# Layer 1's FFN tail: Silu and the activations' high parts written to PSUM, and the second half's norm moved into the FFN tiles

## The chip, the core and the metric

The kernel runs on one core of a Trainium2 chip. Its engines are PE (TensorE, the matmuls; PEld is its weight loading), DVE (VectorE), ACT (ScalarE), POOL (GpSimd) and SP (SyncE, which here only issues transfers). They run side by side and wait for one another through semaphores; each executes its own instructions in the order written. SBUF is the large on-chip memory, PSUM the small one into which PE accumulates; DVE and ACT read and write both. The metric is the time of one execution on the device in microseconds (us), the median over several runs.

## The reference

Two layers of a hybrid attention block over 1024 tokens of width 1024. What matters here is the end of layer 1: the residual after attention's output projection, an RMS norm with gain and shift, and a SwiGLU FFN with inner width 2816 (22 blocks of 128).

```python
def _swiglu(h, wg, wu, wd):
    return (jax.nn.silu(h @ wg) * (h @ wu)) @ wd
...
        x = x + g1 * o
        h = _rms(x, norm2_g[i]) * (1.0 + sc2) + sh2
        x = x + g2 * _swiglu(h, ffn_w_gate[i], ffn_w_up[i], ffn_w_down[i])
```

All of it is float32, and the kernel keeps that precision with split operands.

## The kernel before

**Split matmuls.** Every operand is split into a high part (a cast to a shorter format) and a low part (the source minus the high part). `mm3` multiplies high x high (L74), low x high (L75) and high x low (L76) into one PSUM tile. So each operand costs a cast on ACT, a subtraction and three matmuls for each product. In the rows w_hi, w_lo are a weight's parts, c_hi, c_lo the normed input's, act_hi, act_lo the activations', and h_hi, h_lo (in the program h1_hi, h1_lo, whose room is used again) hold parts of the down weights.

**Layer 1's tail.** The tokens are worked on in two halves (`ci`) of 512. `out_proj1(0)` and `out_proj1(1)` compute the output projection and the residual x, eight output blocks each. `norm1s` is a generator that computes one half's norm in small steps, which other code advances: squares on ACT, their sum (L1285), the reciprocal root (`norm_rstd`), then for each of eight blocks nrm_t (L1293) and nrm_h (L1295). own0 is the first half's, own1 the second's. own0's results go through `combine`, which makes the inputs of a Strassen-like scheme: seven products in place of eight. own1's results are kept in a DRAM tile h_d (L1401) and are read and combined when the second half begins.

**One FFN tile** (`gate_up1`) makes 128 inner columns for 512 tokens. Four weight pieces b11, b12, b21, b22 of gate and up are loaded; POOL makes the sums t1, t2 (L1328, L1329), t3 (L1343) and t4 (L1347). Seven products (`product7`) run in this order, with weights b11, t2, t3, t1, t4, b21, b22. Each is 12 matmuls of 256 columns into a p_ps buffer, of which there are three. For six of the weights `parts_of` casts w_hi on ACT (L1240), copies it to a PSUM tile pmisc on ACT (L1244) and subtracts on DVE (w_lo, L1245), so that DVE reads one operand from SBUF and one from PSUM. b22's w_lo is POOL's. pmisc has two buffers in all. DVE adds the products up into u2, u3, sg and av; ACT applies Silu in place to u3 (L1357) and sg (L1362); DVE multiplies (L1360, L1366); then act_hi is cast on ACT (L1368) and act_lo subtracted on DVE (L1369).

**The down projection.** `down_weights1(f)` loads two pieces on POOL's queue (L1383), casts on ACT (L1384) and subtracts on POOL (L1385). After each even tile from f = 2 to 18, `down1` takes the tiles f - 2 and f - 1: eight output blocks, each six matmuls of 512 columns into a d_ps buffer (three buffers), and DVE adds the result to x (L1394). The last two pairs of a half come after its loop.

**What sets the order.** In this part no order is written by hand: the framework's scheduler takes the program as written and decides each engine's order and the use of the pools' buffers. A tile of a pool can be written when the readers of the tile before it in that buffer are done. The pools here: raw weights 8, w_hi and w_lo 6 each, t 4 (shared with the norm's squares and products), raw down weights 4, act_hi and act_lo 4 each.

Of the kernel before, what the change touches and what calls it, by code (L numbers as in the profile page):

```python
# [9 lines left out]
F32 = mybir.dt.float32  # L10
F32R = mybir.dt.float32r
AF = mybir.ActivationFunctionType
ALU = mybir.AluOpType
# [3 lines left out]
P = 128  # L17
# [46 lines left out]
def build(tc, io):  # L64
    nc = tc.nc
# [3 lines left out]
    def fl(ap):  # L69
        return ap.bitcast(F32)  # L70
# [41 lines left out]
    def vec(l, which):  # L112
        return mod[l][:, which * KT:(which + 1) * KT, :]
# [1110 lines left out]
    wk, wk_cm = pools.open("wk1")  # L1224
# [27 lines left out]
    def out_proj1(ci, ready, own, side=iter(()), then=lambda: None):  # L1252

        h_hi, h_lo = h_out[ci]
        for dt in reversed(range(KT)):
            ws, old = ready
            ready = out_weights(dt - 1) if dt else then()
            ps = pd.tile([P, 512], F32, name="d_ps")
            for k in range(KT):
                hi, lo = ws[k // 4]  # L1260
                mm3(ps, hi[:, k % 4], lo[:, k % 4], h_hi[:, k], h_lo[:, k], k == 0, k == KT - 1)
            cols = slice(ci * 32, ci * 32 + 32)
            for i in range(2):
                rows = slice(8 * i, 8 * i + 8)
                V.scalar_tensor_tensor(
                    x[:, dt, ci * 512:ci * 512 + 512].rearrange("p (c r) -> p c r", r=GH)[:, :, rows],
                    ps.rearrange("p (c r) -> p c r", r=GH)[:, :, rows], vec(1, 2)[:, dt, 0:1],
                    old[i].rearrange("p (r c) -> p r c", c=GW)[:, :, cols].rearrange("p r c -> p c r"),
                    ALU.mult, ALU.add)
            advance(own, 1)  # L1270
            advance(side, 3)
        return ready

    def norm1s(ci, adder, done):


        ts = slice(ci * 512, ci * 512 + 512)
        ss = wk.tile([P, 512], F32, name="nrm_ss")
        for i, k in enumerate(reversed(range(KT))):
            if i == 0:  # L1280
                S.activation(ss, x[:, k, ts], AF.Square)
            else:
                sq = wk.tile([P, 512], F32, name="nrm_sq", tag="t", bufs=4)
                S.activation(sq, x[:, k, ts], AF.Square)
                adder.tensor_tensor(ss, ss, sq, ALU.add)  # L1285
            yield
        for r in norm_rstd(ss, 512, wk, ph):
            yield
        for i in range(4):
            both = []  # L1290
            for k in (i, i + 4):
                t = wk.tile([P, 512], F32, name="nrm_t", tag="t", bufs=4)
                V.scalar_tensor_tensor(t, x[:, k, ts], nA[3][:, k, 0:1], r, ALU.mult, ALU.mult)  # L1293
                h = wk.tile([P, 512], F32, name="nrm_h", tag="wd", bufs=4)
                S.activation(h, t, AF.Identity, bias=vec(1, 3)[:, k, 0:1], scale=1.0)  # L1295
                both.append(h)
                yield
            done(i, *both)
            yield
# [32 lines left out]
    def gate_up1(f, side=iter(()), raws=None):  # L1332
        b11, b12, b22, b21 = raws[:4] if raws else load_gate_up(f)
        t1, t2 = raws[4:] if raws else first_sums(b11, b12, b22)
        t3, t4 = (wk.tile([P, 4, P], F32, name=n, tag="t", bufs=4) for n in ("t3", "t4"))
        p1, u2, u3, sg = (wk.tile([P, HT], F32, name=n) for n in ("p1", "u2", "u3", "sg"))
        av = wk.tile([P, 2, HT], F32, name="av", bufs=2)
        hi, lo = (wk.tile([P, 512], F32R, name=n, bufs=4) for n in ("act_hi", "act_lo"))
        w = parts_of(b11)
        ps = product7(w, 0)  # L1340
        S.copy(p1, ps)
        w = parts_of(t2)
        G.tensor_tensor(t3, b22, b12, ALU.subtract)  # L1343
        ps = product7(w, 4)
        V.tensor_tensor(u2, ps, p1, ALU.add)
        w = parts_of(t3)
        G.tensor_tensor(t4, t2, b21, ALU.subtract)  # L1347
        ps = product7(w, 5)
        V.tensor_tensor(u3, ps, u2, ALU.add)
        w = parts_of(t1)  # L1350
        ps = product7(w, 3)
        V.tensor_tensor(av[:, 1], ps, u3, ALU.add)
        V.tensor_tensor(u2, ps, u2, ALU.add)
        w = parts_of(t4)
        ps = product7(w, 2)
        V.tensor_tensor(u3, u3, ps, ALU.subtract)
        S.activation(u3, u3, AF.Silu)  # L1357
        w = parts_of(b21)
        ps = product7(w, 1)
        V.tensor_tensor(av[:, 1], av[:, 1], u3, ALU.mult)  # L1360
        V.tensor_tensor(sg, ps, p1, ALU.add)
        S.activation(sg, sg, AF.Silu)  # L1362
        w = parts_of(b22, G)
        ps = product7(w, 6)
        V.tensor_tensor(u2, ps, u2, ALU.add)
        V.tensor_tensor(av[:, 0], u2, sg, ALU.mult)  # L1366
        avf = av.rearrange("p a n -> p (a n)")
        S.copy(hi, avf)  # L1368
        V.tensor_tensor(lo, avf, fl(hi), ALU.subtract)  # L1369
        advance(side, 2)  # L1370
        return hi, lo

# [23 lines left out]
                nc.scalar.dma_start(io["out"][:, dt, ts], x[:, dt, ts])  # L1396
            amid(dt)

    def keep(i, h0, h4):
        for k, h in ((i, h0), (i + 4, h4)):  # L1400
            nc.scalar.dma_start(h_d[:, k], h)  # L1401

    own0 = norm1s(0, G, combine)
    ready = out_proj1(0, out_weights(KT - 1), own0, then=lambda: out_weights(KT - 1))
    pools.close(bg_cms[0])
    cc, cc_cm = pools.open("comb", side="right")
    c_hi = cc.tile([P, 7, 4, HT], F32R, name="c_hi")
    c_lo = cc.tile([P, 7, 4, HT], F32R, name="c_lo")
    own1 = norm1s(1, V, keep)
    def first_tile():  # L1410
        raws = load_gate_up(0)
        return *raws, *first_sums(*raws[:3])

    ready = out_proj1(1, ready, own1, own0, then=first_tile)
    advance(own0, 99)
    for ci in range(2):
        acts = {}
        for f in range(NF):
            acts[f] = gate_up1(f, own1 if f else iter(()), ready if f + ci == 0 else None)
            down_weights1(f)  # L1420
            if f % 2 == 0 and 2 <= f < NF - 2:
                down1(ci, (f - 2, f - 1), [acts.pop(f - 2), acts.pop(f - 1)], False)

        h_in = []
        for i in range(4 if ci == 0 else 0):
            if i:
                h_in.append([raw_half(h_d[:, k]) for k in (i, i + 4)])
            else:
                h_in.append([wk.tile([P, 512], F32, name="h_in", tag=t) for t in ("nrm_ss", "nrm_r")])
                for h, k in zip(h_in[0], (0, 4)):  # L1430
                    nc.sync.dma_start(h, h_d[:, k])

        def amid(i):
            if h_in and i in (3, 7, 9, 12):
                combine(4 - len(h_in), *h_in.pop(0), tags=("t", "t"))

        for f in (NF - 4, NF - 2):
            down1(ci, (f, f + 1), [acts.pop(f), acts.pop(f + 1)], f == NF - 2,
                  lambda dt, f=f: amid(dt + (KT if f == NF - 2 else 0)))
# [113 lines left out]
```

## Time and profile before

| | |
|---|---|
| median of 3 runs | 2943.0 us (2942.56 to 2944.94) |
| profiled execution | 2949.19 us, span 2947.4 us |
| mean granted TensorE clock | 0.986 |
| busy over the span | PE 95%, DVE 54%, ACT 41%, POOL 27% |
| layer 1's tail | 2101 to 2947 us |

The profile is of one execution. Rows of groups give a source line, engine, operation, output and inputs with shapes and the count; then busy time and the mean length of one in ns; then the engine's idle time just before these instructions and what ended most of it. Rows of the timeline give the start and length of one instruction, and in brackets the idle time before it. Two successive matmuls overlap, so PE's rate is read from their starts. Two tiles and one down projection (a pair, or unit) repeat through the tail.

### The profile page before, as it was taken

What the parts mean: (1) busy time and instruction counts of PE and PEld (TensorE: products, weight loads), DVE (VectorE), ACT (ScalarE), POOL (GpSimd) and SP (SyncE); (2) the same over time, 40 slices, a digit from 0 to 9 for tenths busy, and PEclk for the clock granted to TensorE, in tenths of its full rate; (3) what the DMA queues carried; (4) which work ended last, traced back from release to release, by engine and by line L of the source; (5) the groups of instructions that cost most, each with busy time, mean ns of one, the idle gap of its engine ahead of it and who ended that gap; (6) DMA issues with size and microseconds to landing.
All of it is one profiled execution on the core that took longest, in us unless ns stands there. A gap on an engine that the chain in (4) does not pass through costs nothing. (4 is left out here: it accounts for less than half of the span.)

```text
span 2947.4 us, 44547 instructions
## 1 busy us (share of the span) xinstructions
PE 2812.9 (95%) x16874; PEld 2350.1 (80%) x16874; DVE 1592.2 (54%) x3144; ACT 1219.9 (41%) x2402; POOL 799.0 (27%) x870
## 2 busy tenths in 40 slices
PE   7989999999999999999989999999989899989999
PEld 5876768888888888888857778777768788888898
DVE  5775553633323333333575252566566777877776
ACT  4345552421111111111253231566447666666664
POOL 1122332000000000000130001455246666676662
PEclk9989999999999999999989999999999999999999
DMA  7236564211011110110124335876343322233231
GB/s 277 85 118 231 213 210 148 65 43 36 29 50 36 36 43 29 43 43 29 54 79 142 108 105 153 186 182 145 117 150 118 128 98 100 99 136 100 97 104 47
DMA packets 149349, 310.59 MB, mean 105 GB/s; under 512 B 13424, under 2 KB 71280, under 8 KB 142096
## 3 DMA queue, kind: packets, MB, share of 16 engines
q1 hardware_dynamic: 133664, 265.73, 28.9%
q0 software_dynamic: 8992, 31.40, 3.3%
q10 hardware_dynamic: 6480, 10.63, 1.0%
q8 instruction: 133, 2.18, 0.3%
q14 instruction: 80, 0.66, 0.1%
HBM read 264.58 MB, written 43.12 MB: 104 GB/s over the span
## 5 line engine op out<-in xcount | busy, mean ns | idle before, releaser
L74 PE MATMUL p_ps<-c_hi,w_hi 128*128 128x256 f32 x1232 | 344.6, 280 | 13.6 <-ACT w_hi L1240 4.6
L76 PE MATMUL p_ps<-c_hi,w_lo 128*128 128x256 f32 x1232 | 343.0, 279 | 4.5 <-DVE w_lo L1245 3.5
L75 PE MATMUL p_ps<-c_lo,w_hi 128*128 128x256 f32 x1232 | 342.7, 278 | 0.0
L810 POOL TENSOR_TENSOR nrm_ss<-nrm_ss,nrm_sq 128x512 f32<-128x512 f32 (+1 forms) x31 | 39.4, 1271 | 1012.9 <-PE d_ps L76 935.4
L775 ACT CAST w_hi<-w_raw 128x1024 fp32r<-128x1024 f32 x106 | 110.5, 1051 | 485.1 <-PE d_ps L75 270.4
L74 PEld LDWEIGHTS p_ps<-c_hi,w_hi 128*128 128x128 f32 x1232 | 233.7, 190 | 17.5 <-ACT w_hi L1240 6.6
L76 PEld LDWEIGHTS p_ps<-c_hi,w_lo 128*128 128x128 f32 x1232 | 233.5, 190 | 5.8 <-DVE w_lo L1245 4.5
L75 PEld LDWEIGHTS p_ps<-c_lo,w_hi 128*128 128x128 f32 x1232 | 233.6, 190 | 0.9
L580 POOL TENSOR_SCALAR pr<-pr,st 128x640 f32<-128x640 f32 (+2 forms) x208 | 156.9, 755 | 266.7 <-DVE st L579 176.8
L878 DVE SCALAR_TENSOR_TENSOR x<-d_ps,mod,x 128x512 f32<-128x512 f32 (+1 forms) x240 | 157.6, 661 | 125.2 <-PE d_ps L76 125.2
L776 DVE TENSOR_TENSOR w_lo<-w_raw,w_hi 128x1024 fp32r<-128x1024 f32 x102 | 124.1, 1224 | 184.0 <-ACT w_hi L775 181.6
L862 DVE TENSOR_TENSOR sg<-sg,u_ps 128x512 f32<-128x512 f32 (+1 forms) x66 | 39.6, 599 | 322.4 <-PE u_ps L76 322.4
L74 PE MATMUL d_ps<-act_hi,w_hi 128*128 128x512 f32 (+1 forms) x528 | 188.8, 358 | 3.5 <-DVE x L878 3.4
L75 PE MATMUL d_ps<-act_lo,w_hi 128*128 128x512 f32 (+1 forms) x528 | 188.7, 357 | 1.3 <-DVE act_lo L864 1.3
L75 PE MATMUL u_ps<-o_lo,w_hi 128*128 128x512 f32 (+1 forms) x528 | 189.3, 358 | 0.0
L76 PE MATMUL u_ps<-o_hi,w_lo 128*128 128x512 f32 (+1 forms) x528 | 189.1, 358 | 0.0
L74 PE MATMUL u_ps<-o_hi,w_hi 128*128 128x512 f32 (+1 forms) x528 | 189.0, 358 | 0.0
L76 PE MATMUL d_ps<-act_hi,w_lo 128*128 128x512 f32 (+1 forms) x528 | 188.9, 358 | 0.0
L74 PE MATMUL g_ps<-o_hi,w_hi 128*128 128x512 f32 (+1 forms) x528 | 188.2, 357 | 0.0
L75 PE MATMUL g_ps<-o_lo,w_hi 128*128 128x512 f32 (+1 forms) x528 | 188.2, 356 | 0.0
L76 PE MATMUL g_ps<-o_hi,w_lo 128*128 128x512 f32 (+1 forms) x528 | 188.2, 356 | 0.0
L574 ACT ACTIVATE pr<-sm,st 128x640 f32<-128x640 f32 (+4 forms) x208 | 162.9, 783 | 31.1 <-POOL sm L563 22.3
(329 smaller groups left out, 7494.6 us busy)
## 6 DMA issues: line engine op xcount, KB each, us to landing
ada_w<-ada_w SPq DMA_DIRECT2D x48, 1024.0 KB, 4.9
wd_raw<-w_down POOLq DMA_DIRECT2D x88, 256.0 KB, 2.9
w_raw<-w_gate SPq DMA_DIRECT2D x88, 256.0 KB, 2.6
w_raw<-w_up SPq DMA_DIRECT2D x88, 256.0 KB, 2.7
k<-k_d SPq DMA_DIRECT2D x28, 640.0 KB, 10.5
w_raw<-w_in SPq DMA_DIRECT2D x24, 512.0 KB, 4.0
w_raw<-w_gate SPq DMA_DIRECT2D x22, 512.0 KB, 3.5
w_raw<-w_up SPq DMA_DIRECT2D x22, 512.0 KB, 3.5
```

The costliest lines, as they stand in the source:

```text
L74: TE.matmul(out, lh, rh, start=first, stop=False)
L75: TE.matmul(out, lh, rl, start=False, stop=False)
L76: TE.matmul(out, ll, rh, start=False, stop=last)
L574: S.activation(self.pr[:, :n], self.sm[:, :n], AF.Exp, bias=st[:, 0:1], scale=-1.0, accum_out=st[:, 1:2])
L580: G.tensor_scalar(self.pr[:, :n], self.pr[:, :n], st[:, 3:4], 0.0, ALU.mult, ALU.add)
L775: S.copy(hi, raw)
L776: eng.tensor_tensor(lo, raw, fl(hi), ALU.subtract)
L810: adder(i).tensor_tensor(ss, ss, sq, ALU.add)
L862: V.tensor_tensor(sg[:, :n], sg[:, :n], u_ps[:, :n], ALU.mult)
L878: V.scalar_tensor_tensor(xs, self.shaped(ps[:, :n]), vec(l, 5)[:, dt, v:v + 1], xs, ALU.mult, ALU.add)
```

## The change

Three things are edited.

First, in `gate_up1` both Silus write to pmisc tiles in PSUM, and the two products that make av read them from there. act_hi is copied to a further pmisc tile by ACT (`first`), and act_lo is computed from the copy. So a tile asks for nine pmisc tiles, where it asked for six; the two buffers remain.

Second, own1 is not advanced in `out_proj1(1)` any more, only in the FFN tiles from f = 1 on, two steps a tile. Its sums and its products are POOL's (they were DVE's), the gain is applied as the scale of ACT's nrm_h, nrm_h gets one buffer of its own, and each result is written to h_d at once.

Third, the down weights of f = 0 are fetched and split together with those of f = 1.

```diff
@@ -1271,7 +1271,7 @@
             advance(side, 3)
         return ready
 
-    def norm1s(ci, adder, done):
+    def norm1s(ci, tag, bufs, each, done):
 
 
         ts = slice(ci * 512, ci * 512 + 512)
@@ -1282,7 +1282,7 @@
             else:
                 sq = wk.tile([P, 512], F32, name="nrm_sq", tag="t", bufs=4)
                 S.activation(sq, x[:, k, ts], AF.Square)
-                adder.tensor_tensor(ss, ss, sq, ALU.add)
+                G.tensor_tensor(ss, ss, sq, ALU.add)
             yield
         for r in norm_rstd(ss, 512, wk, ph):
             yield
@@ -1290,9 +1290,13 @@
             both = []
             for k in (i, i + 4):
                 t = wk.tile([P, 512], F32, name="nrm_t", tag="t", bufs=4)
-                V.scalar_tensor_tensor(t, x[:, k, ts], nA[3][:, k, 0:1], r, ALU.mult, ALU.mult)
-                h = wk.tile([P, 512], F32, name="nrm_h", tag="wd", bufs=4)
-                S.activation(h, t, AF.Identity, bias=vec(1, 3)[:, k, 0:1], scale=1.0)
+                h = wk.tile([P, 512], F32, name="nrm_h", tag=tag, bufs=bufs)
+                if ci:
+                    G.tensor_tensor(t, x[:, k, ts], r, ALU.mult)
+                else:
+                    V.scalar_tensor_tensor(t, x[:, k, ts], nA[3][:, k, 0:1], r, ALU.mult, ALU.mult)
+                S.activation(h, t, AF.Identity, bias=vec(1, 3)[:, k, 0:1], scale=nA[3][:, k, 0:1] if ci else 1.0)
+                each(k, h)
                 both.append(h)
                 yield
             done(i, *both)
@@ -1354,19 +1358,23 @@
         w = parts_of(t4)
         ps = product7(w, 2)
         V.tensor_tensor(u3, u3, ps, ALU.subtract)
-        S.activation(u3, u3, AF.Silu)
+        s2 = ph.tile([P, 512], F32, name="pmisc")[:, 0:HT]
+        S.activation(s2, u3, AF.Silu)
         w = parts_of(b21)
         ps = product7(w, 1)
-        V.tensor_tensor(av[:, 1], av[:, 1], u3, ALU.mult)
+        V.tensor_tensor(av[:, 1], av[:, 1], s2, ALU.mult)
         V.tensor_tensor(sg, ps, p1, ALU.add)
-        S.activation(sg, sg, AF.Silu)
+        s1 = ph.tile([P, 512], F32, name="pmisc")[:, 0:HT]
+        S.activation(s1, sg, AF.Silu)
         w = parts_of(b22, G)
         ps = product7(w, 6)
         V.tensor_tensor(u2, ps, u2, ALU.add)
-        V.tensor_tensor(av[:, 0], u2, sg, ALU.mult)
+        V.tensor_tensor(av[:, 0], u2, s1, ALU.mult)
         avf = av.rearrange("p a n -> p (a n)")
         S.copy(hi, avf)
-        V.tensor_tensor(lo, avf, fl(hi), ALU.subtract)
+        first = ph.tile([P, 512], F32, name="pmisc")
+        S.copy(first, fl(hi))
+        V.tensor_tensor(lo, avf, first, ALU.subtract)
         advance(side, 2)
         return hi, lo
 
@@ -1396,28 +1404,29 @@
                 nc.scalar.dma_start(io["out"][:, dt, ts], x[:, dt, ts])
             amid(dt)
 
-    def keep(i, h0, h4):
-        for k, h in ((i, h0), (i + 4, h4)):
-            nc.scalar.dma_start(h_d[:, k], h)
-
-    own0 = norm1s(0, G, combine)
+    def nothing(*a):
+        pass
+
+    own0 = norm1s(0, "wd", 4, nothing, combine)
     ready = out_proj1(0, out_weights(KT - 1), own0, then=lambda: out_weights(KT - 1))
     pools.close(bg_cms[0])
     cc, cc_cm = pools.open("comb", side="right")
     c_hi = cc.tile([P, 7, 4, HT], F32R, name="c_hi")
     c_lo = cc.tile([P, 7, 4, HT], F32R, name="c_lo")
-    own1 = norm1s(1, V, keep)
+    own1 = norm1s(1, "nrm_ss", 1, lambda k, h: nc.scalar.dma_start(h_d[:, k], h), nothing)
     def first_tile():
         raws = load_gate_up(0)
         return *raws, *first_sums(*raws[:3])
 
-    ready = out_proj1(1, ready, own1, own0, then=first_tile)
+    ready = out_proj1(1, ready, iter(()), own0, then=first_tile)
     advance(own0, 99)
     for ci in range(2):
         acts = {}
         for f in range(NF):
             acts[f] = gate_up1(f, own1 if f else iter(()), ready if f + ci == 0 else None)
-            down_weights1(f)
+            if f:
+                for i in range(0 if f == 1 else f, f + 1):
+                    down_weights1(i)
             if f % 2 == 0 and 2 <= f < NF - 2:
                 down1(ci, (f - 2, f - 1), [acts.pop(f - 2), acts.pop(f - 1)], False)
 
```

The scheduler moves far more than the edits. Three places show it, all in the first half's tiles. Numbers behind names tell tiles of one name apart.

The first is POOL, from the end of a down block in the repeating units. Before, with the current tile's pieces w_raw_21186 to 21192 (b22 is 21190), the next tile's 21362 to 21368 and the one after that 21602 to 21608:

```order
L1385 TENSOR_TENSOR h1_hi_14611<-wd_raw_21774,h1_hi_14611 128x512
L1383 DMA wd_raw_22190<-w_down 128x512
L1245 TENSOR_TENSOR w_lo_21334<-w_raw_21190,w_hi_21333 128x512
L1328 TENSOR_TENSOR t1_21610<-w_raw_21604,w_raw_21602 128x512
L1329 TENSOR_TENSOR t2_21611<-w_raw_21606,t1_21610 128x512
L1343 TENSOR_TENSOR t3_21614<-w_raw_21606,w_raw_21604 128x512
L1347 TENSOR_TENSOR t4_21615<-t2_21611,w_raw_21608 128x512
```

After, with the current tile's pieces 22078 to 22084 (b22 is 22082) and the next tile's 22258 to 22264:

```order
L1393 TENSOR_TENSOR h1_hi_14611<-wd_raw_22678,h1_hi_14611 128x512
L1391 DMA wd_raw_23098<-w_down 128x512
L1332 TENSOR_TENSOR t1_22266<-w_raw_22260,w_raw_22258 128x512
L1391 DMA wd_raw_23102<-w_down 128x512
L1333 TENSOR_TENSOR t2_22267<-w_raw_22262,t1_22266 128x512
L1347 TENSOR_TENSOR t3_22270<-w_raw_22262,w_raw_22260 128x512
L1351 TENSOR_TENSOR t4_22271<-t2_22267,w_raw_22264 128x512
L1245 TENSOR_TENSOR w_lo_22228<-w_raw_22082,w_hi_22227 128x512
```

Before, b22's w_lo came first and the four t's were those of the tile after the next; now the t's are the next tile's, and the current b22's w_lo comes behind them.

The second is ACT in the same tiles, from the casts of the t's on. Before (current tile u3_21202, sg_21203; the t's 21370 to 21375 are the next tile's):

```order
L1240 CAST w_hi_21403<-t2_21371 128x512
L1244 COPY pmisc_21406<-w_hi_21403 128x512
L1240 CAST w_hi_21424<-t3_21374 128x512
L1244 COPY pmisc_21427<-w_hi_21424 128x512
L1240 CAST w_hi_21445<-t1_21370 128x512
L1244 COPY pmisc_21448<-w_hi_21445 128x512
L1357 ACTIVATE u3_21202<-u3_21202 128x256
L1240 CAST w_hi_21466<-t4_21375 128x512
L1244 COPY pmisc_21469<-w_hi_21466 128x512
L1362 ACTIVATE sg_21203<-sg_21203 128x256
L1240 CAST w_hi_21487<-w_raw_21368 128x512
L1244 COPY pmisc_21490<-w_hi_21487 128x512
```

After (current tile u3_22094, sg_22095; the t's 22266 to 22271 are the next tile's, w_hi_22204 is the current b21):

```order
L1240 CAST w_hi_22299<-t2_22267 128x512
L1240 CAST w_hi_22320<-t3_22270 128x512
L1240 CAST w_hi_22341<-t1_22266 128x512
L1362 ACTIVATE pmisc_22202<-u3_22094 128x256
L1244 COPY pmisc_22207<-w_hi_22204 128x512
L1240 CAST w_hi_22362<-t4_22271 128x512
L1368 ACTIVATE pmisc_22225<-sg_22095 128x256
L1240 CAST w_hi_22384<-w_raw_22264 128x512
L1374 CAST act_hi_22097<-av_22096 128x512
L1376 COPY pmisc_22247<-act_hi_22097 128x512
L1244 COPY pmisc_22282<-w_hi_22279 128x512
```

In both, three casts of the next tile's t's stand ahead of the first Silu. Before, each cast is followed by its copy to pmisc; now the next tile's copies come only after act_hi and its copy, and the current tile's b21 is copied behind the Silu.

The third is POOL in tile 2, where own1's sums are made (nrm_ss; w_raw_19464 to 19470 are tile 3's pieces, w_raw_19218 is tile 2's b22). After:

```order
L1332 TENSOR_TENSOR t1_19472<-w_raw_19466,w_raw_19464 128x512
L1285 TENSOR_TENSOR nrm_ss_19193<-nrm_ss_19193,nrm_sq_19386 128x512
L1333 TENSOR_TENSOR t2_19473<-w_raw_19468,t1_19472 128x512
L1285 TENSOR_TENSOR nrm_ss_19193<-nrm_ss_19193,nrm_sq_19389 128x512
L1347 TENSOR_TENSOR t3_19476<-w_raw_19468,w_raw_19466 128x512
L1351 TENSOR_TENSOR t4_19477<-t2_19473,w_raw_19470 128x512
L1393 TENSOR_TENSOR h1_hi_14611<-wd_raw_19828,h1_hi_14611 128x512
L1245 TENSOR_TENSOR w_lo_19364<-w_raw_19218,w_hi_19363 128x512
```

None of the nrm_ss rows was on POOL before. A subtraction for the down weights (L1393, L1385 before) stands ahead of b22's w_lo here, as it does in every second tile of the units after the change.

## The prediction, on record before the changed kernel was run

> **What bounds the kernel now.** I first read the page's busy line, then a table of time stretches, because only layer 1's tail (2101 us to the end at 2947) is touched.
>
> ```profile
> PE 2812.9 (95%) x16874; PEld 2350.1 (80%) x16874; DVE 1592.2 (54%) x3144; ACT 1219.9 (41%) x2402; POOL 799.0 (27%) x870
> ...
> 2186.00:2206.00 20.00, 14.20 (x60) 10.73 (x58) 16.28 (x25) 10.42 (x18) 11.83 (x12) 1.00 0.52 172
> 2206.00:2222.00 16.00, 10.19 (x46) 9.09 (x47) 9.12 (x15) 11.30 (x22) 14.87 (x12) 0.57 0.36 120
> 2270.00:2300.00 30.00, 24.87 (x139) 21.22 (x138) 22.55 (x37) 18.98 (x37) 21.67 (x20) 0.89 0.39 131
> 2300.00:2340.00 40.00, 32.74 (x215) 29.37 (x214) 31.35 (x42) 22.19 (x42) 26.40 (x27) 0.91 0.42 139
> 2412.78:2444.46 31.68, 30.49 (x219) 27.99 (x217) 23.67 (x40) 20.85 (x39) 20.66 (x19) 1.00 0.30 101
> 2741.93:2773.61 31.68, 30.50 (x218) 28.00 (x217) 23.65 (x40) 20.86 (x39) 20.65 (x19) 1.00 0.30 101
> ```
>
> The columns are stretch, length, busy time of PE, PEld, DVE, ACT and POOL (instructions in brackets), granted clock, DMA share, GB/s. PE is busy 95% of the span. The two last rows are one repeating unit of the FFN, a pair of tiles with one down-projection block: 31.68 us in both halves, PE busy 30.49. The first four are the irregular places: out_proj1's end and the first tiles, where PE idles 5.8 of 20, 5.8 of 16, 5.1 of 30 and 7.3 of 40 us, and the clock drops to 0.57, 0.89 and 0.91.
>
> Then single matmuls in the timeline (start, length) give PE's issue rate, and one wait gives the only idle time of the unit:
>
> ```profile
> 2202.01 0.39 PE L76 MATMUL d_ps<-h_hi,w_lo 128*128 128x512 f32 x1
> 2204.11 0.40 PE L76 MATMUL d_ps<-h_hi,w_lo 128*128 128x512 f32 x1
> ...
> 2206.34 0.28 PE L74 MATMUL p_ps<-c_hi,w_hi 128*128 128x256 f32 x1
> 2207.25 0.28 PE L76 MATMUL p_ps<-c_hi,w_lo 128*128 128x256 f32 x1
> ...
> 2459.30 0.39 PE L76 MATMUL d_ps<-act_hi,h_hi 128*128 128x512 f32 x1
> 2460.88 0.50 PE L74 MATMUL d_ps<-act_hi,h_hi 128*128 128x512 f32 x1 [1.19 <-DVE x L1394]
> ```
>
> The first two starts lie nine 512-wide matmuls apart, 0.233 us each; the next two eight 256-wide ones, 0.114 each. A unit has 168 narrow and 48 wide: 19.2 + 11.2 = 30.4 us. The rest, 1.3 us, is the gap at 2460.88: the fourth d_ps buffer waits for x on DVE, which stands behind av and act_lo.
>
> The groups by line over six units (2364 to 2555; busy, mean ns, idle before) give every price used below:
>
> ```profile
> L1366 DVE TENSOR_TENSOR av<-u,sg 128x256 f32<-128x256 f32 x12 | 15.0, 1250 | 1.2
> L1361 DVE TENSOR_TENSOR sg<-p_ps,p 128x256 f32<-128x256 f32 x12 | 4.9, 410 | 0.0
> L1360 DVE TENSOR_TENSOR av<-av,u 128x256 f32<-128x256 f32 x12 | 8.3, 693 | 0.0
> L1368 ACT CAST act_hi<-av 128x512 fp32r<-128x512 f32 x13 | 8.1, 623 | 10.5 <-DVE av L1366 10.5
> L1369 DVE TENSOR_TENSOR act_lo<-av,act_hi 128x512 fp32r<-128x512 f32 x13 | 9.0, 692 | 1.1
> L1244 ACT COPY pmisc<-w_hi 128x512 f32<-128x512 f32 x72 | 42.6, 592 | 2.3
> L1240 ACT CAST w_hi<-t 128x512 fp32r<-128x512 f32 x48 | 29.7, 618 | 2.0 <-PE p_ps L75 1.0
> L1245 DVE TENSOR_TENSOR w_lo<-t,pmisc 128x512 fp32r<-128x512 f32 x48 | 32.9, 685 | 6.0 <-ACT pmisc L1244 5.7
> L1365 DVE TENSOR_TENSOR u<-p_ps,u 128x256 f32<-128x256 f32 x12 | 5.0, 415 | 0.0
> L1357 ACT ACTIVATE u<-u 128x256 f32<-128x256 f32 x12 | 5.0, 418 | 0.3
> L1384 ACT CAST h_lo<-wd_raw 128x512 fp32r<-128x512 f32 x12 | 7.5, 622 | 19.9 <-PE d_ps L75 19.5
> L1385 POOL TENSOR_TENSOR h_lo<-wd_raw,h_lo 128x512 fp32r<-128x512 f32 x12 | 15.6, 1297 | 15.5 <-ACT h_lo L1384 15.4
> L1383 POOL DMA_DIRECT2D wd_raw<-w_down x24 | 13.3, 556 | 7.1 <-POOL h_lo L1385 2.4 <-POOL h_hi L1385 2.1 <-PE p_ps L76 1.8
> L1328 POOL TENSOR_TENSOR t<-w_raw 128x512 f32<-128x512 f32 x11 | 14.3, 1303 | 13.7 <-DVE w_lo L1245 13.7
> L1343 POOL TENSOR_TENSOR t<-w_raw 128x512 f32<-128x512 f32 x11 | 16.3, 1486 | 0.0
> L1245 POOL TENSOR_TENSOR w_lo<-w_raw,w_hi 128x512 fp32r<-128x512 f32 x13 | 17.4, 1335 | 11.0 <-ACT w_hi L1240 5.4 <-PE p_ps L75 5.4
> ```
>
> POOL is only 65% busy there, and its t's are never waited for. With two SBUF operands av takes 1.25 us, with one in PSUM sg takes 0.41.
>
> **The change part by part.** *Silu and act_hi's copy through PSUM.* Both av products get a PSUM operand, so I price them at sg's 0.41. The new copy, same shape as L1244, costs ACT 0.59, and act_lo waits for it. Taken alone the chain av, act_hi, (copy), act_lo goes from 1.25 + 0.62 + 0.69 = 2.56 to 0.41 + 0.62 + 0.59 + 0.69 = 2.31: 0.25 less. But three more tiles per FFN tile (nine instead of six) take turns in the two PSUM buffers of pmisc. The scheduler answers with another order, shown ahead of this section: now the PSUM copies of a tile's weights come only after the previous tile's act_hi copy, so the w_lo's are made in their own tile, not one tile ahead. POOL's t's reuse buffers which those w_lo's free; they were made two tiles ahead and are now made one ahead. They lie on the path.
>
> Three waits follow in a unit; I add each against what PE can do meanwhile.
>
> *First, from the last down matmul.* PE has five products (60 x 0.114 = 6.84), then 4 narrow (b21's and b22's first ones, which need only w_hi), 6 wide (the next block's, for the older tile) and 2 narrow ones of the next tile: 0.46 + 1.40 + 0.23, in all 8.9 us, until b22's w_lo is needed. POOL meanwhile: cast of the freed weight 0.62 (it starts 0.2 before the end), two h_lo subtractions 2.60, DMA issue 0.56, t1 1.30, DMA issue 0.56, t2 1.30, t3 1.49, t4 1.30, b22's w_lo 1.34: 10.9. ACT, whose w_hi of the next tile's t3 and t1 now stand ahead of the Silu, comes out the same: t3 ends at 8.2, then 0.62 + 0.62 + 0.42 + 0.59 and b21's w_lo 0.69 give 11.1. PE waits 11.1 - 8.9 = 2.2.
>
> *Second, at that tile's end*, u 0.42, av 0.41, act_hi 0.62, copy 0.59, act_lo 0.69 and five hand-overs of 0.05 (from the end of the first row below to the start of the second, 2206.07 to 2206.12): 3.0 us. PE holds 4 narrow and 6 wide matmuls against it, 1.86. It waits 1.1.
>
> ```profile
> 2205.39 0.68 DVE L1245 TENSOR_TENSOR w_lo<-w_raw,pmisc 128x512 fp32r<-128x512 f32 x1
> ...
> 2206.12 0.38 PE L76 MATMUL p_ps<-c_hi,w_lo 128*128 128x256 f32 x1 [1.38 <-DVE w_lo L1245]
> ```
>
> *Third, in the other tile*, an h_lo subtraction stands ahead of b22's w_lo on POOL and waits for a down matmul: 0.4 (rest of the cast) + 1.30 + 1.34 = 3.05 after it. PE has 6 wide and 10 narrow: 2.54. It waits 0.5.
>
> The sum is 3.8 us idle for 1.3 now, +2.5 a unit. Units with a down block inside the loops: f = 2, 4 .. 18, nine in each half: 18 x 2.5 = **+45 us**. The first two of these share own1's work, below.
>
> *The deferred down weights and the norm's sums in out_proj1(1).*
>
> ```profile
> 2209.94 0.58 PE L74 MATMUL p_ps<-c_hi,w_hi 128*128 128x256 f32 x1 [2.41 <-ACT w_hi L1240]
> ...
> 2211.13 2.53 POOL L1385 TENSOR_TENSOR h_hi<-wd_raw,h_hi 128x512 fp32r<-128x512 f32 x2 [0.22 <-ACT h_hi L1384]
> 2213.61 1.71 POOL L1343 TENSOR_TENSOR t<-w_raw 128x512 f32<-128x512 f32 x1
> ...
> L1285 DVE TENSOR_TENSOR nrm_ss<-nrm_ss,nrm_sq 128x512 f32<-128x512 f32 x7 | 5.5, 789 | 1.5 <-ACT nrm_sq L1284 1.4
> ```
>
> In tile 0 PE waits for w_hi (2.41 us here), ACT for POOL's t3 (L1343), and that stood behind four h_hi subtractions for f = 0, the last two in the second row. The four casts and four subtractions now come a tile later, where nothing asks for them before the first down block; their DMA issues stay where they were, among own0's sums on POOL's queue. Of own1, seven sums of 0.79 leave DVE in out_proj1(1); its products x.r were inside the FFN tiles already and only change engine there. The idle time from 2186 to 2222 is 5.8 + 5.8, the clock's part 16 x 0.43 = 6.9. The first half of the idle time hangs on own0's c_lo, which stays. So the bounds are 0 and 18; I take the second half and most of the clock, **-12**.
>
> *An act_lo that was stuck.*
>
> ```profile
> 2325.34 7.60 DVE L1369 TENSOR_TENSOR act_lo<-av,act_hi 128x512 fp32r<-128x512 f32 x1
> 2331.12 1.27 POOL L1385 TENSOR_TENSOR h_hi<-wd_raw,h_hi 128x512 fp32r<-128x512 f32 x1
> ...
> 2326.15 0.40 PE L76 MATMUL d_ps<-act_hi,h_hi 128*128 128x512 f32 x1
> 2333.66 0.79 PE L74 MATMUL d_ps<-act_hi,h_hi 128*128 128x512 f32 x1 [7.12 <-DVE x L1394]
> ...
> L810 POOL TENSOR_TENSOR nrm_ss<-nrm_ss,nrm_sq 128x512 f32<-128x512 f32 (+1 forms) x31 | 39.4, 1271 | 1012.9 <-PE d_ps L76 935.4
> ```
>
> An act_lo with two SBUF operands took 7.60 us while POOL worked without a pause; PE waited 7.12 for x behind it, and slow matmuls followed (0.79 for 0.40; 0.09 x 40 = 3.6 us in that stretch). With the copy in PSUM I count this as gone: **-10** (bounds 0 and -11).
>
> *The norm inside the tiles.* Seven sums come to POOL, none is there in the tail now; the older sum of the same shape, 1.27 us, is nearest. The eight products, as two-operand work like L1328, take 1.30: together 19.3 us on the queue that now sets the first wait. Two sums stand between t1 and t3 of each of tiles 1 to 4. About half falls in the tile with that wait: **+10** (bounds 0 and 19). Eight squares of 0.63 on ACT lie in its idle third of a unit; without that cover they are 5 us more. The eight writes of h_d move with the norm on ACT's queue and are read only before the second half. The gain as ACT's scale is an operand of an nrm_h that is there anyway.
>
> Sum: 45 - 12 - 10 + 10 = +33. The profiled execution took 2949.2, span 2947.4, 6.2 over the median; the differences apply to the median: 2943 + 33 = 2976.
>
> The row of 7.12 idle was followed by slow matmuls, those of 1.19 were not. The Trainium skill's page "TensorE: Matmul & The Clock Gate" (Part 1: The HAM clock gate) says that an idle window of about 3.4 us puts the array back to half rate. By that rule the 2.2 us waits cost no clock, and the trace agrees with both ends; only waits lengthened by two POOL sums, about 4.7, would.
>
> **The rivals.** *POOL keeps up* (faster). Then the unit gains 0.25 and the irregular places their 22: 18 x 0.25 + 22 = 26, 2917. For it: POOL idles 35% of a unit now, and the waits come from adding mean durations. Against: the order puts two subtractions, two DMA issues and four t's between one down block and the next w_lo. It decides when POOL's chain from the block's end falls below 8.9 us, two of ten steps fewer than I count. The Trainium skill's "SBUF — State Buffer" (Who interferes with whom) says that a DVE instruction with two SBUF inputs contends with a GpSimd one, one with at most one does not; av against sg agrees, and this is the rule by which it would be faster.
>
> *The lost lookahead and the gains cancel*: with half of the waits, 18 x 1.25 = 22 against 22 gained; 2943, within 0.2% (what this kernel's measurement can tell).
>
> *The waits grow* (slower still). In tiles 1 to 4 two sums lengthen the first wait to 4.7 us, and a slow stretch like those beside 2290 and 2331 follows, 3.3 to 3.6 us (30 x 0.11, 40 x 0.09): 4 x (2.5 + 3.5) = 24 more, 3000; with the irregular places not gaining their 22 either, 3022.
>
> **How the numbers follow.** Forecast 60%, waits grow 15%, cancel 8%, POOL keeps up 17%. The forecast's own range, with units of +1.8 to +3.2, is 2960 to 2995. The range of 8 in 10 reaches into both sides: 2930 to 3012. Slower: 60 + 15 and a little of the cancelling case, 0.76; same 0.07; faster 0.17.
>
> **What would show it.** Right: units of 34 us with PE busy 30.5 in each; before the b21 and b22 products PE waiting for w_lo from POOL or DVE, and ACT for POOL's t; av at 0.41 in the groups; no act_lo over 1 us; stretches of 2186 to 2222 with less idle PE. Wrong: units of 31.7 or less with POOL idle ahead of its t's, or nrm rows on POOL without PE waiting in tiles 1 to 4.

## The result and the profile after

The changed kernel takes 3022.4 us (median of 4 runs, 3020.3 to 3028.2) against 2942.8 beside it: ratio 1.0274, 95% interval 1.0256 to 1.0292, some 80 us slower. The forecast was 2976, its upper bound 3012. The direction was right; the size was not, and most of the excess does not lie where the prediction's sum has its largest term.

First the stretches of the changed kernel (columns as before): three irregular places, then two units.

```profile
2206.00:2232.00 26.00, 12.91 (x58) 11.59 (x58) 5.72 (x13) 11.09 (x21) 17.20 (x18) 0.67 0.38 132
2249.00:2290.00 41.00, 34.11 (x207) 30.38 (x206) 19.95 (x39) 22.08 (x42) 24.59 (x22) 0.88 0.23 77
2396.00:2412.00 16.00, 11.10 (x62) 9.93 (x61) 3.90 (x10) 6.84 (x13) 7.83 (x7) 0.79 0.29 100
...
2463.13:2497.21 34.08, 32.14 (x218) 28.30 (x217) 21.42 (x40) 21.28 (x41) 19.77 (x19) 1.00 0.28 94
2906.80:2940.75 33.95, 32.01 (x217) 28.21 (x216) 21.41 (x41) 21.32 (x41) 19.77 (x18) 1.00 0.28 94
```

A unit takes 34.08 and 33.95 us in place of 31.68, some 2.3 us more; 34 was predicted. The clock is 1.00 in it. In the irregular places PE is idle 13.1 of 26, 6.9 of 41 and 4.9 of 16 us, and the granted clock falls to 0.67, 0.88 and 0.79. Before, in the same stretches, PE was idle 5.8, 4.6 and 1.2 us at 0.74, 1.00 and 1.00, so they are worse, where the prediction had the first tiles better. The first of them, before:

```profile
2206.00:2232.00 26.00, 20.19 (x134) 19.09 (x135) 17.38 (x31) 19.82 (x38) 20.52 (x16) 0.74 0.33 112
```

The groups by line over three units show that the edited instructions do what was priced:

```profile
L1372 DVE TENSOR_TENSOR av<-u,pmisc 128x256 f32<-128x256 f32 x6 | 2.5, 422 | 0.6
...
L1377 DVE TENSOR_TENSOR act_lo<-av,pmisc 128x512 fp32r<-128x512 f32 x6 | 4.1, 682 | 3.9 <-ACT pmisc L1376 3.9
...
L1240 ACT CAST w_hi<-t 128x512 fp32r<-128x512 f32 x24 | 14.6, 621 | 24.6 <-PE p_ps L76 12.3 <-POOL t L1333 7.7 <-POOL t L1347 2.5
```

av takes 0.42 us (1.25 and 0.69 before), act_lo 0.68, the copy 0.59. But ACT now stands idle 24.6 us ahead of the casts of the t's, 10.2 of it for POOL's t2 and t3; before, in twice as many units, it was 2.0. One row of the page's costliest groups, of the changed kernel and then of the one before:

```profile
L76 PE MATMUL p_ps<-c_hi,w_lo 128*128 128x256 f32 x1232 | 352.8, 293 | 53.7 <-POOL w_lo L1245 42.9
```

```profile
L76 PE MATMUL p_ps<-c_hi,w_lo 128*128 128x256 f32 x1232 | 343.0, 279 | 4.5 <-DVE w_lo L1245 3.5
```

Over the whole tail, matmuls with w_lo now wait 53.7 us, 42.9 of it for POOL; it was 4.5, 3.5 of it for DVE.

In the timeline of one unit, all of PE's waits with the matmuls beside them, and POOL between the last down matmul and the w_lo that PE waits for:

```profile
2698.92 0.39 PE L76 MATMUL d_ps<-act_hi,h_lo 128*128 128x512 f32 x1
2699.95 0.39 PE L76 MATMUL p_ps<-c_hi,w_lo 128*128 128x256 f32 x1 [0.63 <-POOL w_lo L1245]
2700.17 0.28 PE L74 MATMUL p_ps<-c_hi,w_hi 128*128 128x256 f32 x1
...
2703.52 0.40 PE L76 MATMUL d_ps<-act_hi,h_lo 128*128 128x512 f32 x1
2704.30 0.96 PE L74 MATMUL d_ps<-act_hi,h_lo 128*128 128x512 f32 x3 [0.37 <-ACT act_hi L1374]
2705.64 0.50 PE L75 MATMUL d_ps<-act_lo,h_lo 128*128 128x512 f32 x1 [0.38 <-DVE act_lo L1377]
...
2716.95 0.28 PE L76 MATMUL p_ps<-c_hi,w_lo 128*128 128x256 f32 x1
2717.78 0.39 PE L76 MATMUL p_ps<-c_hi,w_lo 128*128 128x256 f32 x1 [0.55 <-POOL w_lo L1245]
...
2689.75 0.39 PE L76 MATMUL d_ps<-act_hi,h_hi 128*128 128x512 f32 x1
...
2689.99 2.54 POOL L1393 TENSOR_TENSOR h_hi<-wd_raw,h_hi 128x512 fp32r<-128x512 f32 x2 [3.94 <-PE d_ps L75]
2692.48 0.56 POOL L1391 DMA_DIRECT2D wd_raw<-w_down  x1
2693.05 1.31 POOL L1332 TENSOR_TENSOR t<-w_raw 128x512 f32<-128x512 f32 x1
2694.29 0.55 POOL L1391 DMA_DIRECT2D wd_raw<-w_down  x1
2694.87 1.30 POOL L1333 TENSOR_TENSOR t<-w_raw,t 128x512 f32<-128x512 f32 x1
2696.12 1.30 POOL L1347 TENSOR_TENSOR t<-w_raw 128x512 f32<-128x512 f32 x1
2697.37 1.30 POOL L1351 TENSOR_TENSOR t<-t,w_raw 128x512 f32<-128x512 f32 x1
2698.61 1.28 POOL L1245 TENSOR_TENSOR w_lo<-w_raw,w_hi 128x512 fp32r<-128x512 f32 x1
```

The waits are the three that were predicted, at the predicted matmuls (the second is two rows, for act_hi at 2704.30 and for act_lo at 2705.64), and POOL's chain has the predicted steps, nine on POOL; the tenth, ACT's cast, was done by the block's end. It ends at 2699.89, 9.9 us after the last down matmul (2689.75 and its 0.233), where the sum had 10.9: POOL starts its next instruction 1.24 to 1.25 us after a subtraction or a sum, not 1.30, and the first subtraction came at once.

### The profile page after: what moved, and what is told of

Read it like the earlier page. It is cut to its first block, busy times and chain, and to the rows that moved or that the text cites. A ratio compares the mean times of both kernels' runs of the same rounds, so it can differ in the third digit from the quotient of the medians.

```text
span 3020.0 us, 44515 instructions
## 1 busy us (share of the span) xinstructions
PE 2856.3 (95%) x16874; PEld 2367.0 (78%) x16874; DVE 1530.6 (51%) x3129; ACT 1233.8 (41%) x2446; POOL 796.4 (26%) x885
## 5 line engine op out<-in xcount | busy, mean ns | idle before, releaser
L76 PE MATMUL p_ps<-c_hi,w_lo 128*128 128x256 f32 x1232 | 352.8, 293 | 53.7 <-POOL w_lo L1245 42.9
L74 PE MATMUL p_ps<-c_hi,w_hi 128*128 128x256 f32 x1232 | 350.7, 288 | 8.4 <-ACT p L1345 5.7
L74 PEld LDWEIGHTS p_ps<-c_hi,w_hi 128*128 128x128 f32 x1232 | 240.8, 195 | 22.9 <-ACT w_hi L1240 8.4
L75 PEld LDWEIGHTS p_ps<-c_lo,w_hi 128*128 128x128 f32 x1232 | 240.5, 195 | 1.0
L1240 ACT CAST w_hi<-t 128x512 fp32r<-128x512 f32 x176 | 106.9, 620 | 188.4 <-PE p_ps L76 71.7
```

Of the source, the lines that this page charges most:

```text
L74: TE.matmul(out, lh, rh, start=first, stop=False)
L75: TE.matmul(out, lh, rl, start=False, stop=False)
L76: TE.matmul(out, ll, rh, start=False, stop=last)
L1240: S.copy(hi, src)
```

## Experiments

Theory A was the prediction's: nine pmisc tiles per FFN tile make the scheduler give up a tile of lookahead, and the waits follow. The rivals: that PSUM operands or ACT's added copy cost by themselves, or that the norm on POOL or the deferred down weights made the excess.

**The PSUM part alone.** The edits of `gate_up1` only.

```diff
+        s2 = ph.tile([P, 512], F32, name="pmisc")[:, 0:HT]
+        S.activation(s2, u3, AF.Silu)
...
+        first = ph.tile([P, 512], F32, name="pmisc")
+        S.copy(first, fl(hi))
+        V.tensor_tensor(lo, avf, first, ALU.subtract)
```

> Only the PSUM part: both Silus and act_hi's copy go through pmisc, norm and down weights stay as before. Theory A (the nine pmisc tiles take the lookahead away and own1 and the deferral are a separate loss): units of 33.95 us as in the changed kernel, 18 of them +2.27 each, +41, less up to 10 for the stuck act_lo: 2974 to 2985. Theory B (the PSUM part alone makes also the early tiles slow, own1 and the deferral cost little): 3005 to 3022. Theory C (the PSUM part is a gain and the norm took it): 2915 to 2940, units of 31.4 or less.

3011.1 us, ratio 1.0223 (1.0206 to 1.0240): +66 us, by theory B's numbers. The unit of this kernel, and three of PE's waits in its early tiles:

```profile
2453.86:2487.93 34.07, 32.15 (x218) 28.33 (x217) 21.42 (x41) 21.30 (x41) 19.77 (x19) 1.00 0.29 93
```

```profile
2282.11 0.58 PE L76 MATMUL p_ps<-c_hi,w_lo 128*128 128x256 f32 x1 [3.75 <-POOL w_lo L1245]
2302.97 0.39 PE L76 MATMUL p_ps<-c_hi,w_lo 128*128 128x256 f32 x1 [2.84 <-POOL w_lo L1245]
2340.96 0.39 PE L76 MATMUL p_ps<-c_hi,w_lo 128*128 128x256 f32 x1 [2.95 <-POOL w_lo L1245]
```

The unit is the changed kernel's, 34.07. In tiles 3 to 6 PE waits 3.75, 2.84 and 2.95 us for b22's w_lo from POOL, without any of own1's sums there. The changed kernel, which has those sums on POOL, has waits for w_lo of 3.31, 3.23 and 3.33 at 2261, 2282 and 2304 us. So these waits, which the prediction put down to the norm in its rival "the waits grow", need only the PSUM part.

**The norm alone, the deferral alone.** The second diff is the deferral.

```diff
-    ready = out_proj1(1, ready, own1, own0, then=first_tile)
+    ready = out_proj1(1, ready, iter(()), own0, then=first_tile)
```

```diff
-            down_weights1(f)
+            if f:
+                for i in range(0 if f == 1 else f, f + 1):
+                    down_weights1(i)
```

> Only the norm part: own1 leaves out_proj1(1), its sums and products go to POOL inside the tiles, gain as scale; Silu, act_lo and the down weights as before. Theory A (own1's sums hurt because POOL is on the path only after the PSUM part): 2943 plus or minus 8, units unchanged at 31.68. Theory B (own1 on POOL is a loss by itself, waits of PE for w_lo from POOL in tiles 1 to 4 followed by slow clock): 2955 to 2970.

> Only the deferral: the down weights of tile 0 are fetched and split with those of tile 1, all else as before. Theory A (eight subtractions in a row on POOL and casts that wait for their DMAs on ACT stand ahead of tile 0's products, as the waits of 5.7 and 6.4 us in the changed kernel suggest): 2950 to 2960. Theory B, as the prediction had it (POOL makes tile 0's t's sooner): 2931 to 2938.

2945.8 us, ratio 1.0000 (0.9991 to 1.0010), and 2944.9, 0.9999 (0.9990 to 1.0008): neither changes the total by itself. A unit with the norm part alone:

```profile
2421.44:2453.10 31.66, 30.49 (x217) 28.00 (x216) 23.64 (x40) 20.82 (x39) 20.60 (x19) 1.00 0.31 100
```

It is the unit of before. The gain of 12 which the prediction gave to these two edits isn't in the total. The deferral moved nothing there. A tile has two subtractions for the down weights, so the four that the prediction saw ahead of t3 and took for those of f = 0 are those of two tiles. With the deferral alone four stand at the same place; the last two and t3 are these:

```profile
2202.88 2.52 POOL L1385 TENSOR_TENSOR h_hi<-wd_raw,h_hi 128x512 fp32r<-128x512 f32 x2 [0.22 <-ACT h_hi L1384]
2205.36 1.72 POOL L1343 TENSOR_TENSOR t<-w_raw 128x512 f32<-128x512 f32 x1
```

For the norm, 1.0000 is a balance and not nothing. The last 60 matmuls of `out_proj1(1)` take 19.1 us before, 16.1 with the deferral alone and 14.0 with the norm alone, which is 60 times 0.233, so PE no longer waits there. But behind them it waits longer than before (2.41 and 2.17 us there):

```profile
2214.36 0.58 PE L74 MATMUL p_ps<-c_hi,w_hi 128*128 128x256 f32 x1 [5.27 <-ACT p L1345]
2224.67 0.58 PE L74 MATMUL p_ps<-c_hi,w_hi 128*128 128x256 f32 x1 [3.05 <-DVE u L1357]
```

**Silu to the free half of the product's own PSUM tile.** A p_ps tile has 512 columns and a product uses 256. Here the Silus write the other half, so pmisc keeps six tiles per FFN tile; act_lo reads SBUF.

```diff
-        ps = product7(w, 2)
+        ps, s2 = product7(w, 2, True)      # s2: columns 256 to 511 of the same tile
...
+        S.activation(s2, u3, AF.Silu)
```

> Silu's results go to the unused second half of the product's own p_ps tile, so DVE's two av products read PSUM but pmisc keeps its six tiles per FFN tile; act_lo reads SBUF as before; norm and down weights as before. Theory A (the order lost its lookahead through pmisc; the PSUM operands themselves are good): the order stays that of before, av falls from 1.25 to about 0.41 us, the one gap of a unit shrinks by up to 0.84 us: 18 x 0.84 = 15 less, 2928 (2920 to 2940). Theory B (PSUM operands or a held p_ps buffer cost time whatever the order): 2943 to 2970 with units of 31.7 or more.

2917.2 us, ratio 0.9902 (0.9887 to 0.9917): 28 us faster than before and 105 faster than the changed kernel, theory A's side and beyond its number.

```profile
2413.82:2444.35 30.53, 30.53 (x217) 28.34 (x217) 22.21 (x41) 20.85 (x39) 20.25 (x19) 1.00 0.32 104
```

```profile
L1367 DVE TENSOR_TENSOR av<-u,p_ps 128x256 f32<-128x256 f32 x44 | 18.5, 420 | 3.9
L1370 DVE TENSOR_TENSOR act_lo<-av,act_hi 128x512 fp32r<-128x512 f32 x44 | 48.7, 1107 | 7.3 <-ACT act_hi L1369 7.1
```

The unit takes 30.5 us, and PE is busy for all of it: the one gap of 1.3 us is gone. The 13 units that run undisturbed in the traces (second and fourth rows of the table below) make 16 us of the gain; the rest lies in the stretches ahead of them and at the change of halves. av takes 0.42 here as in the changed kernel (the groups are those of the whole tail). A PSUM operand is therefore no loss by itself.

**Silu through pmisc without the copy; the copy without Silu.**

```diff
-        S.activation(u3, u3, AF.Silu)
+        s2 = ph.tile([P, 512], F32, name="pmisc")[:, 0:HT]
+        S.activation(s2, u3, AF.Silu)
```

```diff
-        V.tensor_tensor(lo, avf, fl(hi), ALU.subtract)
+        first = ph.tile([P, 512], F32, name="pmisc")
+        S.copy(first, fl(hi))
+        V.tensor_tensor(lo, avf, first, ALU.subtract)
```

> Both Silus write pmisc tiles (eight per FFN tile), act_lo reads SBUF, norm and down weights as before. Its instructions are those of the run with the Silus in the p_ps tile, only the pool differs. Theory A (pmisc's rotation takes the lookahead): no gain of 28 us but a loss; units above 32.5 us, total above 2965, with w_hi copies to pmisc behind the Silus and PE waiting for w_lo. Theory B (act_hi's copy is what hurts, Silu through pmisc does not): 2915 to 2935 as in the p_ps run.

> Only act_hi's copy to a pmisc tile (seven per FFN tile), Silus in place in SBUF. Theory A: the order of this kernel also has the next tile's copies behind act_hi's, so a loss: 2960 to 3010, PE waiting for w_lo in every tile. Theory B (the Silus alone took the lookahead): 2935 to 2950, av still at 1.25 us.

2956.0 us, ratio 1.0042 (1.0026 to 1.0058), and 2950.7, 1.0022 (1.0012 to 1.0033). Both lose, but 12 and 6 us, less than theory A's numbers: its "above 2965" and "units above 32.5" are missed. One unit of each, Silu first:

```profile
2438.44:2469.82 31.38, 31.38 (x219) 28.07 (x218) 22.36 (x42) 19.83 (x39) 20.60 (x19) 1.00 0.32 102
```

```profile
2429.08:2460.67 31.59, 30.68 (x218) 28.13 (x217) 22.07 (x41) 21.21 (x40) 20.03 (x18) 1.00 0.32 100
```

With eight or seven pmisc tiles the units keep 31.4 and 31.6 us; with nine they take 34. So the price doesn't grow by the tile: each of the two edits alone is covered in the units, which are no longer than before, and both together make the 34 us. Silu's loss lies elsewhere: its kernel is 6.6 us longer up to the fourth down block and 4.2 around the change of halves. Why it is the ninth tile was not taken apart. Silu through pmisc has the same instructions as the run with the free half and differs from it by 39 us; only the pool differs.

**The free half, with act_hi's copy through pmisc.**

> Silu in the free half of p_ps (2917 alone) plus act_hi's copy through pmisc (2951 alone, against 2944 before). If the copy takes the lookahead whatever Silu does, the units go from 30.45 back to about 31.6 as with the copy alone: 2917 + 18 x 1.1 = 2937 (2930 to 2950). If the loss needs all nine tiles of pmisc in one FFN tile, the copy costs little and act_lo gets shorter: 2910 to 2922.

2943.2 us, ratio 1.0005 (0.9995 to 1.0014). The copy gives back all that the free half had won.

```profile
2423.64:2455.24 31.60, 30.68 (x218) 28.07 (x217) 21.25 (x41) 21.11 (x40) 20.04 (x18) 1.00 0.30 101
```

The unit is 31.60, that of the copy alone. Nothing of the loss is Silu's here. Is it the copy's own 0.59 us or its pmisc tile? PE's one wait in this unit is for neither the copy nor act_lo:

```profile
2439.84 0.38 PE L76 MATMUL p_ps<-c_hi,w_lo 128*128 128x256 f32 x1 [0.92 <-POOL w_lo L1245]
```

b22's w_lo again stands behind four t's on POOL, which in the free-half kernel come after it. So one more pmisc tile, at the end of the FFN tile, is enough to change the order; a run with the copy in a tile of another pool, which would show it without the trace, was not made.

**The PSUM part, but not at the ends.** Seven tiles around out_proj1's end and the change of halves keep SBUF operands.

```diff
+        psum=(ci, f) not in ((0, 0), (0, 1), (0, 2), (0, 20), (0, 21), (1, 0), (1, 1))
...
+        s2 = ph.tile([P, 512], F32, name="pmisc")[:, 0:HT] if psum else u3
```

> The PSUM part alone, but tiles 0, 1, 2, 20, 21 of the first half and 0 and 1 of the second keep Silu and act_lo in SBUF, as before; these are the tiles around out_proj1's end and the change of halves, outside the 18 repeating units. The PSUM part alone measured 3011, of which 13 units of +2.27 us, seen clean in the trace, make 30 and all 18 would make 41. Theory A (the lost lookahead also costs at these ends, where no full down block hides POOL's chain: +12 up to tile 3, +4 around the change of halves, by the tiles' times): 2990 to 2998. Theory B (the rest of the loss lies in the units of tiles 3 to 11 or comes everywhere): 3005 to 3013.

2988.4 us, ratio 1.0144 (1.0126 to 1.0163): 23 us less than the PSUM part everywhere, on theory A's side and a little below its range. The stretch 2200 to 2290 of this kernel, then of the PSUM part everywhere:

```profile
2200.00:2290.00 90.00, 76.24 (x508) 68.94 (x507) 60.42 (x104) 61.63 (x114) 55.03 (x46) 0.91 0.35 114
```

```profile
2200.00:2290.00 90.00, 70.12 (x423) 61.40 (x422) 47.59 (x88) 55.57 (x101) 43.44 (x36) 0.87 0.29 93
```

508 matmuls run in the same 90 us, against 423. The starts of the last matmuls of the down blocks in the traces show all the places (us of one profiled execution each):

| stretch | before | PSUM part everywhere | not at the ends | changed kernel | free half |
|---|---|---|---|---|---|
| first FFN product to the 4th down block | 168.3 | 189.2 | 177.1 | 194.3 | 162.8 |
| on to the 9th, five units | 158.4 | 170.1 | 170.4 | 178.0 | 152.3 |
| on to the second half's 1st | 107.2 | 118.1 | 107.0 | 120.6 | 98.5 |
| on to its 9th, eight units | 254.0 | 272.3 | 272.1 | 271.5 | 244.0 |
| on to the end | 55.2 | 58.9 | 58.6 | 58.7 | 55.4 |

So 23 of the 66 us come from seven tiles: 12 up to the fourth down block and 11 around the change of halves. Only two of the prediction's 18 units touch these tiles, 4.5 us at 2.27 each; the others are outside its sum. The 13 units of the second and fourth rows make 30 of the 66.

**Combinations.** The PSUM part with the norm, and with the deferral; the free half with both.

> The changed kernel with the down weights of tile 0 back in tile 0. The PSUM part alone measured 3011, all three 3022; norm and deferral alone each 0. If the norm's sums on POOL cost once POOL is on the path: 3018 to 3024. If the deferral costs there (eight subtractions in a row, and ACT's casts waiting for DMAs): 3009 to 3014.

> The PSUM part and the deferral, norm as before; completes the combinations (PSUM part 3011, with the norm 3020, all three 3022). If the two add up: 3011 + 3 = 3014 (3010 to 3017). If the deferral by itself costs what the prediction had as a gain, under the new order: 3020 to 3026. If it gains as predicted: 2999 to 3005.

> Silu in the free half of p_ps together with the norm part and the deferral; act_lo from SBUF. If norm and deferral cost nothing as long as the lookahead is there: 2912 to 2922, the same as the p_ps run alone. If they cost because POOL's queue is on the path in tiles 1 to 11: 2925 to 2935. If the relief of DVE there now shows as a gain, since the units are PE-bound: 2905 to 2911.

3019.6 us, ratio 1.0254 (1.0234 to 1.0274); 3011.7, 1.0227 (1.0211 to 1.0243); and 2917.1, 0.9907 (0.9891 to 0.9922). With the PSUM part the norm adds 8 us and the deferral 1; the half-widths of the two intervals, 5 and 6 us, together leave about 1 to 16 for the norm. With the free half both add nothing. PE's two longest waits at the first tiles in the changed kernel are also in the run without the deferral, shown first:

```profile
2209.21 0.58 PE L74 MATMUL p_ps<-c_hi,w_hi 128*128 128x256 f32 x1 [7.13 <-ACT p L1345]
...
2221.73 0.58 PE L76 MATMUL p_ps<-c_hi,w_lo 128*128 128x256 f32 x1 [5.96 <-POOL w_lo L1245]
```

```profile
2211.57 0.58 PE L74 MATMUL p_ps<-c_hi,w_hi 128*128 128x256 f32 x1 [5.68 <-ACT p L1345]
...
2224.25 0.58 PE L76 MATMUL p_ps<-c_hi,w_lo 128*128 128x256 f32 x1 [6.40 <-POOL w_lo L1245]
...
2207.99 0.62 ACT L1392 CAST h_lo<-wd_raw 128x512 fp32r<-128x512 f32 x1 [1.84 <-DMA wd_raw<-w_down]
2216.75 0.62 ACT L1392 CAST h_lo<-wd_raw 128x512 fp32r<-128x512 f32 x1 [4.71 <-DMA wd_raw<-w_down]
```

In the second fence, the changed kernel, ACT's casts for the down weights wait for their loads (1.84 and 4.71 us) ahead of tile 0's copy p1 and of later casts. Without the norm part, PSUM part and deferral together, the longest wait there is 2.4 us:

```profile
2202.63 0.58 PE L74 MATMUL p_ps<-c_hi,w_hi 128*128 128x256 f32 x1 [2.37 <-ACT w_hi L1240]
```

So neither wait needs the deferral, to which one would put them down by the names in the second fence. The first, for ACT's p, needs only the norm part: it is 5.27 in the run of the norm alone, shown above, where ACT's casts for the down weights wait for their loads too. The second, for POOL's w_lo, is at that place only in the runs with both: with the norm alone the next long wait is 3.05, for DVE.

The norm's 8 us lie mostly elsewhere, in the second row of the table (178.0 against 170.1). There two of own1's products stand ahead of the next tile's t's on POOL, PE waits 4.54 us for b22's w_lo, and the clock falls to 0.79, the third irregular place above. The run without the deferral has the same wait (4.53); the run of the PSUM part alone has none over 1 us in these units:

```profile
2394.44 1.31 POOL L1295 TENSOR_TENSOR nrm_t<-x,nrm_r 128x512 f32<-128x512 f32 x1
2396.28 1.31 POOL L1295 TENSOR_TENSOR nrm_t<-x,nrm_r 128x512 f32<-128x512 f32 x1
...
2405.48 0.80 PE L76 MATMUL p_ps<-c_hi,w_lo 128*128 128x256 f32 x2 [4.54 <-POOL w_lo L1245]
```

## Why the prediction was right and wrong

- *The lost lookahead and its three waits*: right, at the places of the sum. A unit gained 2.27 us (33.95 for 31.68), 2.5 was predicted; 18 such would be 41 us for 45. Only some run clean: in the run of the PSUM part alone 13 units make 30 us, the other five lie in stretches with longer waits. The mechanism is shown by the trace, and by the free-half run, which keeps pmisc's six tiles and has none of these waits.
- *The sizes of the waits*: the first was 2.2 in the sum and is 0.63 by the profile's idle column. That column begins after the 0.39 us which the row gives the matmul before; by starts the gap is 1.03, that is 0.80 over the 0.233 of a wide matmul, and the next start comes 0.1 late. Counted so, the four gaps are 0.80, 0.54, 0.55 and 0.72 with some 0.1 behind each: 3.0 us, where the sum had 3.8: the first was priced too long (0.9 for 2.2), the others too short. With 30.4 of matmuls this leaves half a microsecond to the unit's 33.95, single starts that come some 0.1 late, which the sum did not have. That 2.27 lies so near to 2.5 is therefore partly luck. So PE's busy time of 32.0 (30.5 was to be seen) holds no more work; it is ends of matmuls that no longer lie under the next one.
- *The chain with the copy*: right as a price, and the sentence that a shorter chain would be given away by the order holds: the copy alone, the simplest part, already costs 6 us on the kernel before and 26 on the free-half kernel, where PE's wait in the unit is for POOL's w_lo.
- **The failed step is the deferred down weights, the norm's sums and the stuck act_lo, together -22.** The runs show 0 for each of the first two in the total (0.9999, 1.0000): the deferred casts and subtractions, which were to come a tile later, stay ahead of tile 0's t3, and its wait for w_hi stays (2.37 for 2.41). The norm's gain in `out_proj1(1)` is real, but it is paid back by the waits of 5.27 and 3.05 behind it. What stands in place of the -22 is a loss of some 25 us, the PSUM part's 66 less 18 times 2.27, which the sum did not contain: it counted the lost lookahead for the 18 units only. The run that spares the tiles around out_proj1's end and the change of halves shows the place of most of it, by 23 us, at most 4.5 of them from units. A reason for it, argued and not measured: these tiles have no whole down block beside them, 11.2 us of wide matmuls, under which POOL's chain could lie.
- *The stuck act_lo* (-10): the duration went as predicted, the time did not. The 40 act_lo of this group, all with a PSUM operand, take 0.68 us on average, and 7.60 is gone:

```profile
L1377 DVE TENSOR_TENSOR act_lo<-av,pmisc 128x512 fp32r<-128x512 f32 x40 | 27.3, 683 | 28.7 <-ACT pmisc L1376 28.7
```

The run of the copy alone shows the price without the other edits, since its act_lo has a PSUM operand too (0.69 at most). From the second to the third down block, where the 7.60 was, it takes 34.6 us for 40.6; but on to the fourth it takes 38.6 for 31.7, with a new wait:

```profile
2347.82 0.55 PE L74 MATMUL p_ps<-c_hi,w_hi 128*128 128x256 f32 x1 [4.75 <-DVE sg L1361]
```

From the first product to the fourth down block it is 169.7 us against 168.3. So the time saved at act_lo is lost one unit later, and the term is about 0 here. Two SBUF operands alone don't make act_lo that long either: in the free-half kernel, where it reads SBUF, the longest takes 2.58 us.
- *The norm inside the tiles*, +10 for POOL's 19 us: 8 (1 to 16) with the lost lookahead, 0 without. The size fits, with its condition, that POOL is on the path, but not the place: the sums do not lengthen the early waits for w_lo (3.23 to 3.33 us with them, 2.84 to 3.75 without), two of the products do so later (4.54).
- *The rivals*: "POOL keeps up" fell. "The waits grow" gave 3022 and the kernel measures 3022; that is luck in good part, since its reason was only partly right: the long waits and slow stretches are there (0.67, 0.88, 0.79), in the PSUM part alone too (0.87 over 2200 to 2290), where own1 adds no sum to POOL. The measured parts: 66 from the PSUM part, 8 from the norm, 1 from the deferral, together 75 of the 80; the rest lies within the intervals.
- *The clock*: waits of 0.4 to 0.6 us in units left it at 1.00; those of 5.68 and 6.40 lie in the stretch with 0.67. In the run of the PSUM part alone the narrow matmul after a wait of 3.75 took 0.58, those after 2.84 and 2.95 took 0.39. The Trainium skill's page "TensorE: Matmul & The Clock Gate" (Part 1: The HAM clock gate) gives an idle window of about 3.4 us after which the array runs at half rate; these three waits lie on both sides of it. But the length of one wait doesn't decide here: in the same run a matmul after 2.39 us took 0.58, 3.8 us behind one that had waited 1.40, and in the changed kernel one took 0.58 after 3.23 us and one 0.39 after 3.33. So the prediction's reading that waits of 2.2 cost no clock is not safe; its own row of 2.41 was followed by a matmul of 0.58.

```profile
2206.20 0.58 PE L74 MATMUL p_ps<-c_hi,w_hi 128*128 128x256 f32 x1 [2.39 <-ACT w_hi L1240]
```

```profile
2282.39 0.58 PE L76 MATMUL p_ps<-c_hi,w_lo 128*128 128x256 f32 x1 [3.23 <-POOL w_lo L1245]
```

## What to carry to other kernels

A temporary tile isn't free because its memory is: taken from a small shared pool, it moves everything that takes turns in that pool, and the price is lookahead in places that the edit never names. So look for room that no other tile waits for (here the unused half of a PSUM tile that is held anyway), and compare the order of the instructions before the time. When a steady loop loses its lookahead, count also the places where the loop starts and ends, since what hides the longer chain in the loop is missing there.

## What the runs showed of the hardware that was not expected

The wide spread of a two-operand VectorE instruction beside POOL: in the free-half kernel act_lo, which reads SBUF twice, averages 1.11 us over the tail, with one PSUM operand 0.68, and before one stood for 7.60 while POOL ran six instructions one after another. Yet the kernel with the slower act_lo is the faster: its units have no idle time of PE, so nothing there waits for act_lo. And the idle column of a matmul's row understates a short wait, by 0.17 us in the first gap above and 0.1 behind it. A PSUM tile whose one half PE has filled, and whose other half ACT then fills while the tile is held, brought PE no wait in the units: it has no idle time there.
